# A streaming batch norm in which the third load no longer waits for the second

## Chip, cores, metric

The kernel runs on one core of a Trainium2 chip. The metric is device time in microseconds (us).

## The reference

```python
x: float32 [32, 256, 128, 128]; gamma, beta, running_mean, running_var: float32 [256]
return gamma * (x - mean) / np.sqrt(var + 1e-5) + beta     # one scale and one shift a channel
```

The data are 64 tiles of 128 partitions by 16384 float32, 8.39 MB each. Every tile is read once and written once.

## The kernel before

Three buffers hold three tiles. The sync queue issues the loads, the scalar queue the stores; VectorE computes each tile in place with one instruction. The first tile is loaded in two pieces, so that the parameters can pass between them. This is the part that matters, with cuts marked:

```python
nc.sync.dma_start(out=bufs[0][:, left], in_=xr[0][:, left]).then_inc(early, 16)
# ... four small loads of the parameters ...
nc.sync.dma_start(out=bufs[0][:, right], in_=xr[0][:, right]).then_inc(loaded[0], 16)
for i in range(1, NT):
    s, turn = i % NBUF, i // NBUF                       # NBUF = 3, NT = 64
    if turn:
        nc.sync.wait_ge(stored[s], 16 * turn)           # the buffer must have been stored
    inst = nc.sync.dma_start(out=bufs[s][:], in_=xr[i]).then_inc(loaded[s], 16)
    if i >= 2:                                          # the gate: the load before has landed
        inst._wait_ge(loaded[(i - 1) % NBUF], 16 * ((i - 1) // NBUF + 1))
# ... scale and shift from the parameters ...
compute(0, left)._wait_ge(early, 16)
compute(0, right)._wait_ge(loaded[0], 16)
store(0, 2)
for i in range(1, last):
    compute(i)._wait_ge(loaded[i % NBUF], 16 * (i // NBUF + 1))
    turn_of_store(i)                                    # store i-1 has landed
    store(i, i + 2)
compute(last, slice(0, VCOLS))._wait_ge(loaded[last % NBUF], 16 * turns)
nc.scalar.activation(out=t[:, VCOLS:], in_=t[:, VCOLS:], ...)   # the rest of the last tile
store(last, last + 3)                                   # without turn_of_store
```

## Time and profile before

| | before |
|---|---|
| time, median of 3 runs | 2486.41 us (2485.8 to 2487.24) |
| span in the profile | 2484.7 us |
| bytes moved, mean rate | 1073.84 MB, 432 GB/s |
| load 1 lands, load 2 is issued | 52.85, 52.87 us |
| load 2 lands | 91.50 us |
| store 0 lands (store 1 is issued then) | 69.8 us |
| last load lands, before the end of the span | 30.3 us |

In the lines of the profile q1 is the ring of the loads, q10 that of the stores. A line of the waits gives the total in us, the number of waits and the longest. A line of the timeline gives start, duration, engine or queue, source line and operation. The prediction below shows the lines of before and reads them.

### The profile page before, as it was taken

What the parts mean: (1) busy time and instruction counts of PE and PEld (TensorE: products, weight loads), DVE (VectorE), ACT (ScalarE), POOL (GpSimd) and SP (SyncE); (2) the same over time, 40 slices, a digit from 0 to 9 for tenths busy, and PEclk for the clock granted to TensorE, in tenths of its full rate; (3) what the DMA queues carried; (4) which work ended last, traced back from release to release, by engine and by line L of the source; (5) the groups of instructions that cost most, each with busy time, mean ns of one, the idle gap of its engine ahead of it and who ended that gap; (6) DMA issues with size and microseconds to landing.
All of it is one profiled execution on the core that took longest, in us unless ns stands there. A gap on an engine that the chain in (4) does not pass through costs nothing.

```text
span 2484.7 us, 389 instructions
## 1 busy us (share of the span) xinstructions
DVE 564.0 (23%) x76; ACT 7.9 (0%) x3; POOL 0.2 (0%) x4
## 2 busy tenths in 40 slices
DVE  3121221212212222122221221212212122121221
ACT  0000000000000000000000000000000000000001
POOL 0000000000000000000000000000000000000000
DMA  9999999999999999999999999999999999999999
GB/s 422 423 439 434 430 436 435 437 428 437 435 436 432 433 438 429 436 434 431 434 427 437 437 426 439 436 432 430 436 438 430 433 427 438 430 430 437 436 426 406
DMA packets 18707, 1073.84 MB, mean 432 GB/s; under 512 B 2128, under 2 KB 2192, under 8 KB 2192
## 3 DMA queue, kind: packets, MB, share of 16 engines
q1 hardware_dynamic: 9488, 536.94, 50.1%
q10 hardware_dynamic: 9216, 536.88, 49.9%
q14 instruction: 3, 0.02, 0.0%
HBM read 536.94 MB, written 536.87 MB: 432 GB/s over the span
## 4 chain that ended last, share of the span: by engine, by line
DMA 99%; ACT 0%; SPq 0%; issue 0%; DVE 0%; DVEq 0%
DMA t<-in_x_dram 99%; ACT t L154 0%; SPq L87 0%; DVE rows L85 0%; SPq L91 0%; DVE eps_t L103 0%; DVEq L190 0%; SPq L66 0%
## 5 line engine op out<-in xcount | busy, mean ns | idle before, releaser
L126 DVE TENSOR_SCALAR t<-t,scale_t,shift_t 128x16384 f32<-128x16384 f32 (+2 forms) x65 | 560.5, 8624 | 1886.5 <-DMA t<-in_x_dram 1886.4
L154 ACT ACTIVATE t<-t,shift_t,scale_t 128x7168 f32<-128x7168 f32 x1 | 6.4, 6361 | 2442.7 <-DMA t<-in_x_dram 2442.7
L104 DVE STREAM_TRANSPOSE turned<-rows 32x1024 f32<-32x1024 f32 x1 | 1.2, 1233 | 7.1 <-DMA rows<-in_running_mean_dram 7.1
L111 ACT ACT_TABLE_LOAD x1 | 1.3, 1283 | 0.9 <-SPq L66 0.9
L85 DVE MEMSET rows<- 32x1024 f32 x1 | 0.9, 912 | 1.2 <-SPq L66 1.2
L109 DVE COPY par<-turned 32x8 f32<-32x8 f32 x4 | 0.6, 162 | 0.1
L111 ACT ACTIVATE std_t<-par,eps_t 128x2 f32<-128x2 f32 x1 | 0.3, 295 | 9.2 <-DVE par L109 9.2
L118 DVE RECIPROCAL rstd_t<-std_t 128x2 f32<-128x2 f32 x1 | 0.2, 166 | 0.4 <-ACT std_t L111 0.4
L121 DVE TENSOR_TENSOR shift_t<-par,ms_t 128x2 f32<-128x2 f32 x1 | 0.2, 163 | 0.0
L120 DVE TENSOR_TENSOR ms_t<-par,scale_t 128x2 f32<-128x2 f32 x1 | 0.2, 161 | 0.0
L119 DVE TENSOR_TENSOR scale_t<-par,rstd_t 128x2 f32<-128x2 f32 x1 | 0.2, 161 | 0.0
L179 POOL MEMSET const-bfloat16-1.0<- 128x1 bf16 x1 | 0.1, 102 | 0.0
L179 POOL MEMSET const-uint8-127<- 128x1 uint8 x1 | 0.1, 101 | 0.0
L179 POOL MEMSET const-float32-0.0<- 128x1 f32 x1 | 0.1, 99 | 0.2 <-issue 0.2
L179 POOL MEMSET const-float32-1.0<- 128x1 f32 x1 | 0.1, 98 | 0.0
L103 DVE MEMSET eps_t<- 128x1 f32 x1 | 0.1, 59 | 0.1
## 6 DMA issues: line engine op xcount, KB each, us to landing
t<-in_x_dram SPq DMA_DIRECT2D x1, 6144.0 KB, 19.4
t<-in_x_dram SPq DMA_DIRECT2D x1, 2048.0 KB, 7.6
out_dram<-t ACTq DMA_DIRECT2D x64, 38.6
t<-in_x_dram SPq DMA_DIRECT2D x63, 38.6
rows<-in_running_var_dram SPq DMA_DIRECT2D x1, 16.0 KB, 6.4
rows<-in_gamma_dram SPq DMA_DIRECT2D x1, 16.0 KB, 6.2
rows<-in_beta_dram SPq DMA_DIRECT2D x1, 16.0 KB, 5.9
rows<-in_running_mean_dram SPq DMA_DIRECT2D x1, 16.0 KB, 5.9
```

The lines of the kernel that those rows point to most:

```text
L85: zeroed = step(nc.vector.memset(rows[:], 0.0))
L103: step(nc.vector.memset(eps_t[:], eps))
L104: step(nc.vector.transpose(out=turned[:], in_=rows[:]), fetched, 16 * NPAR)
L109: placed = step(nc.vector.tensor_copy(out=flat[q * B : (q + 1) * B], in_=blocks[:, :, q, 0]))
L111: nc.scalar.activation(out=std_t[:], in_=var_t, func=mybir.ActivationFunctionType.Sqrt, bias=eps_t[:], scale=1.0,)._wait_ge(vec, placed).t ...
L118: step(nc.vector.reciprocal(out=rstd_t[:], in_=std_t[:]), act, 1)
L119: step(nc.vector.tensor_mul(out=scale_t[:], in0=gamma_t, in1=rstd_t[:]))
L120: step(nc.vector.tensor_mul(out=ms_t[:], in0=mean_t, in1=scale_t[:]))
L121: ready = step(nc.vector.tensor_sub(out=shift_t[:], in0=beta_t, in1=ms_t[:]))
L126: return nc.vector.tensor_scalar(out=t[:, cols], in0=t[:, cols], scalar1=scale_t[:, cb : cb + 1], scalar2=shift_t[:, cb : cb + 1], op0=myb ...
L154: nc.scalar.activation(out=t[:, VCOLS:], in_=t[:, VCOLS:], func=mybir.ActivationFunctionType.Identity, bias=shift_t[:, cb : cb + 1], scale ...
L179: nc = _bacc.Bacc("TRN2", target_bir_lowering=False, num_devices=1)
```

## The change

Only loads into a buffer used before keep the gate: from load 3 (the fourth tile) on a load waits for the one ahead of it, while load 2 is queued directly behind load 1. The intent is to take a gap out of the ramp without giving up one transfer a ring in the steady state.

```diff
             inst = nc.sync.dma_start(out=bufs[s][:], in_=xr[i]).then_inc(loaded[s], 16)
-            if i >= 2:
+            if turn:
                 inst._wait_ge(loaded[(i - 1) % NBUF], 16 * ((i - 1) // NBUF + 1))
```

## The prediction

> **What bounds the kernel now.** I read the page first, then the chain of waits, the sync queue's own waits, the timeline of the first 180 us, and last the transfer records cut into stretches of one microsecond around 50 us.
>
> From the page:
>
> ```profile
> span 2484.7 us, 389 instructions
> DVE 564.0 (23%) x76; ACT 7.9 (0%) x3; POOL 0.2 (0%) x4
> ...
> DMA  9999999999999999999999999999999999999999
> GB/s 422 423 439 434 430 436 435 437 428 437 435 436 432 433 438 429 436 434 431 434 427 437 437 426 439 436 432 430 436 438 430 433 427 438 430 430 437 436 426 406
> ...
> q1 hardware_dynamic: 9488, 536.94, 50.1%
> q10 hardware_dynamic: 9216, 536.88, 49.9%
> ...
> DMA t<-in_x_dram 99%; ACT t L154 0%; SPq L87 0%; DVE rows L85 0%; SPq L91 0%; DVE eps_t L103 0%; DVEq L190 0%; SPq L66 0%
> ```
>
> The reader should see three things. The 16 transfer engines are busy in every one of the forty slices, while VectorE works 23% of the span. The two rings, q1 with the loads (sync queue) and q10 with the stores (scalar queue), take half of the engines each. And the chain that ended last is the loads alone, one after another. So the kernel is a stream of 1073.84 MB, and the time is those bytes by the rate, plus what is at the two ends.
>
> The sum, to know how much could be won at all. In the chain of waits the landings of two loads are most often 38.63 us apart; in that time one 8.39 MB tile is loaded and one is stored, 16.78 MB / 38.63 us = 434 GB/s. 64 tiles by 38.63 us are 2472.3 us. Before the first bytes lie 2.0 us and after the last ones some 3 us (the last stretches with traffic end at about 2481.5 us). The loads from 91.50 to 2454.41 us took 61 periods in 2362.91 us, where 61 x 38.63 would be 2356.4: some dozen periods were 38.8 to 39.4 us long, 6.5 us in all. 2472.3 + 2.0 + 3 + 6.5 = 2483.8, against a span of 2484.7. About 1 us is left over: the engines have no hole anywhere in which a saving could lie, in the ramp either.
>
> **The wait that the change removes.** The sync queue's own waits in the first 60 us, then the same kind of view for the whole span, then lines of the timeline:
>
> ```profile
> SPq L98 <- DMA t<-in_x_dram: 48.0, 1, 48.0
> ```
>
> ```profile
> SPq L98 <- DMA t<-in_x_dram: 1378.8, 62, 48.0
> SPq L97 <- DMA out_dram<-t: 1009.0, 61, 16.8
> ```
>
> ```profile
> 52.87 0.33 SPq L98 DMA_DIRECT2D t<-in_x_dram  x1
> ...
> 69.77 0.34 ACTq L137 DMA_DIRECT2D out_dram<-t  x1
> ...
> 91.52 0.33 SPq L98 DMA_DIRECT2D t<-in_x_dram  x1
> ```
>
> Load 2 (the third tile) waits 48.0 us for load 1 to land, at 52.85 us, and is issued at 52.87. It is the only one of the 62 waits at L98 that the change removes; 48.0 us looks large, but the sync queue has nothing else to do in them, and the engines were at work. Store 0 is issued at 30.04 us, lands at 69.7, and store 1 follows at once.
>
> What the wait costs the load ring is seen only in the transfer records. These are 16 packets of the load ring from 47 to 48 us, 16 of the store ring from 54 to 55 us, and the traffic from 44 to 62 us in forty slices of 0.45 us:
>
> ```profile
> q1 hardware_dynamic: 16, 1.05, 241.8%
> ```
>
> ```profile
> q10 hardware_dynamic: 16, 1.05, 241.8%
> ```
>
> ```profile
> GB/s 0 728 1602 0 0 0 146 2039 146 0 0 0 1602 728 0 0 0 728 1602 0 0 0 146 2039 146 0 0 0 1456 874 0 0 0 437 1893 0 0 0 0 1893
> ```
>
> 16 packets that take 241.8% of 16 engines' microsecond are 2.418 us each, of 65,536 bytes (1.05 MB / 16). The bursts of the last line, 2.4 us apart, are packets being booked where they end, all 16 engines in step. So time here comes in slots of 2.42 us, one packet per engine; a tile is 8 slots, and 16 slots are 38.7 us, the period. Going through the one-microsecond stretches, the slots end: load data 47.5, store 49.9, store 52.4 (with 16 empty packets of q1 in 51 to 53 us: load 1's semaphore), store 54.7, load 57. After its last data packet the load ring thus sits out two slots more than in plain turns: one in which the semaphore packet takes its turn, and one because load 2 is not yet in the ring at 52.4 us. In both the store ring moves a full packet on every engine.
>
> **What the Trainium skill says.** "DMA: Bandwidth & Descriptors", section "Queues, rings and completion order": each engine goes round-robin between the rings that have work, a packet at a time. This trace agrees, with alternating slots of 2.42 us where both have work, and one ring's packets alone where not. The same page, "Issuing engines are not separate DMA queues": transfers of the sync and scalar queues run on the same 16 engines and interleave; q1 at 50.1% and q10 at 49.9% say so too. Its section "Where 436 GB/s comes from" gives a ceiling of 435.2 GB/s; the 434 GB/s measured here lie 0.3% below. Its "Anatomy of one DMA" puts about 2 us of fixed cost on a transfer, mostly completion; that fits a semaphore that arrives a slot after the data, and it is a cost of the ring, not of the engines, as long as the other ring has packets.
>
> **The change, part by part.** It removes one wait, in one instruction; the instruction streams of all engines have the same rows in the same order in both kernels. The wait of load 2 alone goes; loads 3 to 63 keep both waits.
> 1. Load 2 is issued about 0.4 us after load 1, at some 4.8 us, rather than 52.87. Until load 1's data are done nothing changes: the load ring serves load 1 first.
> 2. At 52.4 us the load ring has a packet ready and takes the slot that store 0 has now. Gain for the load ring: 1 slot, 2.4 us. Loss for store 0: 1 slot, 2.4 us. Sum over the engines: 0.
> 3. Load 2 lands at 91.50 - 2.4 = 89.1 us, and store 0 at 69.7 + 2.4 = 72.1. Each ring starts its next transfer when its last has landed, so the shift stays: every later load lands 2.4 us earlier and every later store 2.4 us later than before.
> 4. Does this open a hole? Load 3 needs store 0 (72.1) and load 2 (89.1): the load still comes last. In the steady state the slack of the store wait was 21.8 us (the load landed that long after it); it becomes 21.8 - 4.8 = 17.0. Store 2 needs tile 2 computed (89.1 + 8.8 = 97.9) and store 1 landed (108.5 + 2.4 = 110.9): still no wait for VectorE. No hole.
> 5. The end: the last load lands at 2452.0 instead of 2454.4, the ScalarE and VectorE halves are done 6.4 us later, at 2458.4, and the last store enters the ring while store 62 still moves (it landed at 2464.1 before, and would at about 2466.5). Store 62 and 63 have then one slot more to move alone after the loads end. The 2.4 us won on the loads are handed back here, in full. Change of the end: 0.
>
> The sum is 0 us; I take off 0.1 us for one handover less, an allowance and no measurement, and predict 2486.3 us.
>
> **The rivals.** First: the slot is really saved, because the engines idle somewhere while the load ring is empty. It would make the time 2484.0 us. For it: the share of the engines swings from 0.15 to 1.5 in stretches of 2 us; but that is packets being booked in bursts, and from 52.85 to 91.50 us, which holds both gaps, 16.78 MB moved at 434 GB/s, as later. Against it too: after 2464 us the store ring alone moves a tile in 19.3 us, 434 GB/s, so one ring fills the engines. Second: the shift is harmful. If loads that ran ahead met a buffer not yet stored, each period would get longer; there are 17 us of slack by step 4, so nothing should come of it. Two loads queued in one ring could also spread the 16 engines apart, so that a transfer ends with its slowest engine and each handover costs more: half a slot in each of 61 periods would be 74 us, 3%. But load 1 was already queued directly behind the rest of tile 0, and the engines are in step within 1 us around 50 us. Third: the dozen long periods depend on how the two rings stand to each other; with none of them the time is 6.5 us less, with twice as many 6.5 us more. Nothing ties them to the phase, and I give it little weight.
>
> **Range and chances.** The three runs of before lie within 1.4 us; the first rival takes 2.4 us off; another sample of long periods may move 1 or 2 us. So 2484.0 to 2489.0 us. 2% are 50 us; nothing that the change touches is that large for the faster side, as only 12 us of the span are not packets at full rate. The slower side keeps a little for engines out of step.
>
> **What would show it.** In the changed kernel: the wait of 48.0 us at L98 gone and that line's waits 61; load 2 landing 2 to 3 us earlier and store 0 that much later; the wait for the store longer by about 5 us at each tile and for the load shorter by as much; the last load 2.4 us earlier and the span within 1.5 us. The prediction is wrong if the span falls by 2.4 us with the last load (then a slot was idle), if the periods differ from 38.6 us, or if the store ring does not lose the slot.

## The result, and the profile after

The changed kernel took 2485.47 us (median of 6 runs, 2483.91 to 2487.61) against 2486.11 us for before (6 runs, 2483.59 to 2487.33). The ratio is 0.9999, with a 95% interval of 0.9986 to 1.0012: the same. The interval is some 3 us wide to either side, so the times alone would not show a slot of 2.4 us, won or lost; that is left to the traces. Here and below a ratio is the mean time of one kernel's runs over that of the other's of the same rounds, so not quite the ratio of the medians quoted. Executions over 1.5% slower than the fastest of the same kernel are left out of the means.

From the page of the changed kernel:

```profile
span 2485.8 us, 389 instructions
...
DMA t<-in_x_dram 96%; DMA out_dram<-t 2%; DVE t L126 0%; ACT t L154 0%; SPq L87 0%; DVE rows L85 0%; DVE eps_t L103 0%; DVEq L190 0%; SPq L97 0%; SPq L66 0%
```

The bound is unchanged: the chain is still transfers end to end. It now passes through store 0 at its start, because load 3 waits for that store's landing before it waits for load 2. The profiled run of this kernel happened to be its slowest of six, so the 1.1 us between the two spans are not an effect.

**The ramp.** Timeline of the changed kernel, and then the two lines of before that the prediction does not show:

```profile
72.45 0.34 ACTq L137 DMA_DIRECT2D out_dram<-t  x1
...
89.36 0.33 SPq L98 DMA_DIRECT2D t<-in_x_dram  x1
...
111.16 0.34 ACTq L137 DMA_DIRECT2D out_dram<-t  x1
...
130.31 0.33 SPq L98 DMA_DIRECT2D t<-in_x_dram  x1
```

```profile
108.46 0.34 ACTq L137 DMA_DIRECT2D out_dram<-t  x1
...
130.20 0.33 SPq L98 DMA_DIRECT2D t<-in_x_dram  x1
```

Each issue follows the landing that it waits for by 0.02 to 0.1 us. Store 0 lands 2.7 us later than before (72.4 against 69.8) and load 2 lands 2.2 us earlier (89.34 against 91.50): one slot of 2.42 us has gone from one ring to the other. But load 3 lands at 130.29 us, 0.1 us later than before. In this pair of traces the lead in absolute time was gone after one tile (the second pair, below, differs).

Where it went is seen in the transfers. First the changed kernel from 54 to 55 us, where before 16 store packets stood; then the changed kernel from 93 to 94.2 us, and the kernel before from 92.9 to 94 us:

```profile
q1 hardware_dynamic: 14, 0.92, 211.6%
```

```profile
q1 hardware_dynamic: 13, 0.85, 164.0%
q10 hardware_dynamic: 3, 0.20, 48.0%
```

```profile
q10 hardware_dynamic: 16, 1.05, 219.8%
```

At 54 us the load ring takes the slot that store 0 had (the other two of its 16 packets start just after 55). At 93 us, the handover from load 2 to load 3, 13 engines already have a load packet and 3 do not: these take one more store packet. The engines have fallen into two groups. Load 3 has landed only when the slower group is done, so it lands nearly a slot late, and store 2 likewise (issued and landed 40.9 us apart instead of 38.7). The missed turn alone does not explain the delay. If each packet's end is joined to the start that follows it within 5 ns, the records can be followed engine by engine: the three engines make up the turn, with as many slots for load 3 as most of the others, but some of their packets take longer (on one of them 3.42, 2.76 and 3.12 us instead of 2.42; on another a store packet of 4.23). Why they do stays open.

**The steady state and the end.** The sync queue's waits over the whole span, after and then the two last of before:

```profile
SPq L97 <- DMA out_dram<-t: 1350.8, 61, 67.0
SPq L98 <- DMA t<-in_x_dram: 1035.6, 61, 19.2
SPq L164 <- DMA out_dram<-t: 50.4, 1, 50.4
SPq L66 <- DMA out_dram<-t: 19.3, 1, 19.3
```

```profile
SPq L164 <- DMA out_dram<-t: 48.0, 1, 48.0
SPq L66 <- DMA out_dram<-t: 19.3, 1, 19.3
```

The wait for the load is now 1035.6 / 61 = 17.0 us a tile; before it was (1378.8 - 48.0) / 61 = 21.8. The wait for the store grew from 1009.0 / 61 = 16.5 to (1350.8 - 67.0) / 60 = 21.4. So the two rings stand two slots otherwise to each other, through the whole run. At the end ScalarE starts on the last tile when its load has landed; before, then after:

```profile
2454.43 6.36 ACT t L154
```

```profile
2453.21 6.36 ACT t L154
```

From there to the end of the span are 2484.7 - 2454.4 = 30.3 us before and 2485.8 - 2453.2 = 32.6 us after. The store ring has one slot more to do alone. The slot that the load ring won is paid back at the end.

### The profile page after: what moved, and what is told of

It is laid out like the page before. It is cut to its first block, busy times and chain, and to the rows that moved or that the text cites. A ratio compares the mean times of both kernels' runs of the same rounds, so it can differ in the third digit from the quotient of the medians.

```text
span 2485.8 us, 389 instructions
## 1 busy us (share of the span) xinstructions
DVE 564.1 (23%) x76; ACT 7.9 (0%) x3; POOL 0.2 (0%) x4
## 4 chain that ended last, share of the span: by engine, by line
DMA 98%; another core or an unknown queue 1%; DVE 0%; ACT 0%; issue 0%; SPq 0%; DVEq 0%
DMA t<-in_x_dram 96%; DMA out_dram<-t 2%; DVE t L126 0%; ACT t L154 0%; SPq L87 0%; DVE rows L85 0%; DVE eps_t L103 0%; DVEq L190 0%; SPq L97 0%; SPq L66 0%
## 6 DMA issues: line engine op xcount, KB each, us to landing
out_dram<-t ACTq DMA_DIRECT2D x64, 38.6
t<-in_x_dram SPq DMA_DIRECT2D x63, 38.6
```

## Experiments

Twelve kernels ran; each was correct. Each group shared its runs of the kernel before. Edits are shown against the kernel before, with cuts marked.

### Controls: both kernels once more

Edit: none.

> The kernel before, unchanged, as a control. All theories: ratio 1.000, and single runs within 2483.5 to 2488. It tells how large a difference has to be before a time can show it, and whether the store lands 17 us after the load in a second trace too.

> The changed kernel, unchanged, for a second trace. Theory (the slot of 2.42 us passes from the store ring to the load ring and is handed back at the end): within 1.5 us of before; load 2 lands at 89 to 90 us, store 0 at 72 to 73, and the last load lands about 31 us before the end of the span instead of 30.3 less a slot. Rival (a slot is saved for good, and the first trace hid it by chance): 2.4 us faster. If the 3 engines that missed their turn at load 3 in the first trace are chance, load 3 lands at 127.8 us here; if they are the rule, at about 130.3 again.

| | median us | runs | ratio, 95% interval |
|---|---|---|---|
| kernel before, shared | 2484.04 | 9 | |
| before_again | 2484.28 | 5 | 0.9998 (0.9984 to 1.0011) |
| after_again | 2484.67 | 5 | 0.9999 (0.9987 to 1.0012) |

The handover from load 2 to load 3 in the second trace of the changed kernel:

```profile
89.22 0.33 SPq L98 DMA_DIRECT2D t<-in_x_dram  x1
...
128.54 0.33 SPq L98 DMA_DIRECT2D t<-in_x_dram  x1
```

And the landing of load 3 in the second trace of the kernel before:

```profile
131.43 0.33 SPq L98 DMA_DIRECT2D t<-in_x_dram  x1
```

Load 2 and store 0 (72.3 us) do the same as in the first trace. Load 3 lands at 128.5 us, between the two values expected: from 93 to 94.2 us, 10 engines took a load packet and 6 a store packet. In a third trace with the same ramp (slow_tail_after below) it was 13 and 3 again. So the split at load 3 is in all three traces of this ramp, and its size varies. The kernel before is not free of it: in its first trace 14 load and 2 store packets start from 56 to 58 us, where load 2 begins, and had caught up when load 2 landed; in its second trace two engines lag at load 3, which lands at 131.4 us, 1.2 us later than in the first. Pair by pair, load 3 of the changed kernel is then 0.1 us late, 2.9 us early here, and 1.0 us early in the slow tails (129.2 against 130.1). What does not vary is the relation of the rings: from the last load's landing to the end of the span, 2484.1 - 2453.8 = 30.3 us in before_again and 2482.8 - 2450.1 = 32.7 us here. The rival of a slot saved for good is out.

### slow_tail_before, slow_tail_after: let the end hang on the last load

ScalarE alone computes the last tile, so that the last store comes after the store ring has run empty. The same edit on both kernels:

```diff
-        compute(last, slice(0, VCOLS))._wait_ge(loaded[last % NBUF], 16 * turns)
         nc.scalar.activation(
-            out=t[:, VCOLS:],
-            in_=t[:, VCOLS:],
+            out=t[:],
+            in_=t[:],
...
-        store(last, last + 3)
+        store(last, last + 2)
```

> The kernel before, with ScalarE alone computing the last tile, about 14.5 us instead of 6.4: the last store is issued some 4 us after the store ring has run empty. Theory: the end now hangs on the last load's landing; about 7 us longer than before, 2491 to 2495.

> The same with the changed kernel. Theory: the load ring's one slot of lead, handed back at the end otherwise, is now seen: 2.4 us (1 to 4) less than the same tail on the kernel before, about 2489 to 2492. Rival (the lead of 2.4 us does not live to the end): the same time as with the tail on the kernel before.

With this tail the kernel before took 2489.55 us (5 runs, 2488.23 to 2490.42; ratio 1.0021, 1.0007 to 1.0034) and the changed kernel 2487.30 us (5 runs, 2486.74 to 2489.48; ratio 1.0014, 1.0000 to 1.0029). The wait between the landings of the last two stores, which was 19.3 us in both, first with the kernel before and then with the changed one:

```profile
SPq L66 <- DMA out_dram<-t: 25.1, 1, 25.1
```

```profile
SPq L66 <- DMA out_dram<-t: 22.7, 1, 22.7
```

The hole at the end is 25.1 - 19.3 = 5.8 us in one and 22.7 - 19.3 = 3.4 us in the other: a difference of one slot, 2.4 us. The medians differ by 2.25 us, the means by 1.7; the traces are the firmer of the two. The total for the kernel before was lower than the 2491 us expected at least, as ScalarE took 14.04 us and the hole was 5.8 us, not 7. The lead does live to the end, and is worth 2.4 us in a kernel whose end hangs on its last load. In the real kernel the end hangs on bytes.

### gate_first: put a wait where nothing else can fill it

```diff
-            if i >= 2:
+            if i >= 1:
```

> Load 1 too waits for the load before it, at 23.3 us, when no store is in the store ring yet (store 0 is issued at 30 us). Theory (a wait costs what the engines stand idle): a hole from the last packet of tile 0 to the first of load 1, about 1.5 to 3.5 us, and the whole run that much longer: 2487.5 to 2490. Rival (a wait between two loads costs nothing, or one slot, wherever it is): 0, or 2.4 us, and no stretch without traffic at 23 to 26 us in the trace.

It took 2488.83 us (5 runs, 2487.49 to 2491.0; ratio 1.0019, 1.0007 to 1.0032). The traffic from 20 to 30 us in slices of 0.25 us, of the kernel before and then of this one:

```profile
GB/s 0 0 1180 1769 197 0 0 0 0 1049 2359 786 0 0 0 0 0 0 0 1573 2621 0 0 0 0 0 0 0 524 1835 1835 0 0 0 0 0 0 0 1049 2359
```

```profile
GB/s 0 0 1573 1573 0 0 0 0 0 0 0 0 0 0 0 0 2097 1573 262 0 262 0 0 0 0 0 0 0 262 2884 1049 0 0 0 0 0 0 0 1311 2359
```

The packets are booked where they start. The last packet of tile 0 starts at 20.5 to 21 us in both. By the records the first of load 1 follows at 22.36 us before and only at 24.15 us here: a hole of about 1.8 us. It is the same kind of wait as the one that the change removed, ahead of the neighbouring load, and it costs time because the store ring is empty until 30 us. The time rose by 4.8 us between the medians, more than the hole. Another 0.6 us are at the end, where the last store waited 19.9 us instead of 19.3, and in the records the first packets of load 1 take 3.14 us on average instead of 2.42, which is 0.7 us more. These 3.1 us are about what the span of this trace, 2487.1 us, lies above the two traces of before (2484.7 and 2484.1); the rest of the 4.8 us is not accounted for (see the next run).

### hold_part: hold load 2 back further, beside a busy store ring

```diff
-            if i >= 2:
+            if i == 2:
+                inst._wait_ge(done, 3)
+            elif i > 2:
                 inst._wait_ge(loaded[(i - 1) % NBUF], 16 * ((i - 1) // NBUF + 1))
...
+            if i == 1:
+                compute(1, slice(0, 6144))._wait_ge(loaded[1], 16)
+                compute(1, slice(6144, HW))
+            else:
+                compute(i)._wait_ge(loaded[i % NBUF], 16 * (i // NBUF + 1))
```

(The counts of `done` that later stores wait for go up by one.)

> Load 2 is held back further: it waits until a first part of tile 1 has been computed, 3.3 us after load 1 has landed. Theory: the store ring fills the slots (store 0 lands one or two slots earlier, load 2 one or two later, at 93 to 97 us), no hole, the time within 1.5 us of before. Rival (the wait of load 2 lies on the path to the end): 3.3 us or one to two slots, 2.4 to 4.8 us, longer.

It took 2487.74 us (6 runs, 2484.73 to 2499.62) against 2484.30 us; ratio 1.0022, 1.0003 to 1.0042. Timeline, and the last wait:

```profile
64.94 0.34 ACTq L139 DMA_DIRECT2D out_dram<-t  x1
...
96.51 0.33 SPq L98 DMA_DIRECT2D t<-in_x_dram  x1
```

```profile
SPq L66 <- DMA out_dram<-t: 19.9, 1, 19.9
```

Store 0 lands 4.8 us earlier than in before (two slots) and load 2 lands 5.0 us later, as the theory has it. The time missed what it expected: the medians differ by 3.4 us, which by size would fit the rival. The trace does not show where 3.4 us would lie. Its span is 2484.9 us, against 2484.7 and 2484.1 in the two traces of before, with traffic in every slice and 0.6 us at the end. It does not rule a loss out either: the runs of before in the same rounds had spans of 2481.2 to 2484.4 us. The slowest runs, one of them at 2499.62 us, were not profiled. In this kernel and in gate_first the stores land about 12 us after the loads (706.8 / 61 and 714.1 / 61 us of wait for the store), not 17 or 22. The next runs show that this distance can matter; that it costs 2 to 3 us here is not shown and stays open.

### no_gate: take the gate away altogether

```diff
-            if i >= 2:
-                inst._wait_ge(loaded[(i - 1) % NBUF], 16 * ((i - 1) // NBUF + 1))
```

> No load waits for the load before it; loads 3 to 63 wait for their buffer's store alone. Theory (engines always have a packet, so who waits in a ring does not matter): loads run ahead by one slot a tile until the store of the buffer holds them, and the time stays within 3 us of before. Rival one (each gap in the load ring costs a slot of the span): 61 gaps less, up to 61 x 2.42 = 148 us faster, 6%. Rival two (when the store's landing starts both the next load and the next store, both rings are empty at once): a hole of about 2 us a tile, some 50 x 2 = 100 us slower, 4%.

It took 3225.88 us (5 runs, 3216.49 to 3232.75): ratio 1.2983 (1.2960 to 1.3006), 30% slower. No theory had this size. From its page, and then its transfers from 60 to 150 us alone:

```profile
GB/s 418 432 361 315 337 322 319 348 317 336 315 339 323 316 337 314 341 317 357 322 319 338 314 345 319 334 316 315 336 315 350 314 335 317 326 336 315 340 317 360
...
q1 hardware_dynamic: 9488, 536.94, 47.8%
q10 hardware_dynamic: 9216, 536.88, 40.9%
```

```profile
DMA packets 656, 38.80 MB, mean 431 GB/s; under 512 B 64, under 2 KB 64, under 8 KB 64
```

The rate is full for the first two slices and then falls to some 330 GB/s for good. In the full-rate part a second load is queued behind the first about half of the time (from 5 to 53, 72 to 89, 113 to 126 and 155 to 162 us). From 72 us on each landing of a store releases the next load and the next store together. At first an earlier load is then still in the ring; the rate falls from 204 us on, when the loads have run so far ahead that this ring too is empty at that moment (the load landed at 203.85 us, the store at 204.0). Two things are added up in the 740 us. The engines stand without work for 100 - 47.8 - 40.9 = 11% of the span, some 360 us, about half. And the single packets take longer: in the trace's records from 204 us on, load packets average about 3.06 us and store packets 2.58 us where they were 2.42 us.

### store_two_back: release a load and a store together another way

```diff
             if turn:
-                nc.sync.wait_ge(stored[s], 16 * turn)
+                nc.sync.wait_ge(stored[(i - 2) % NBUF], 16 * ((i - 2) // NBUF + 1))
```

> Each load from the fourth on waits for the store two tiles back, not three, as if there were two buffers. The load and the next store are then released by the same landing, when both rings have run empty. Theory (a wait costs only when both rings are empty): a hole of 1.5 to 3 us at each of some 61 tiles, 2580 to 2670 us, 4 to 7% slower. Rival (the engines' work is what counts and waits do not matter): within 2%.

It took 3000.51 us (median of 4; 2876.7, 3002.09, 3005.1 and 2998.92), beyond the 7% expected. Only the first of these counts as fast, so no ratio was formed; at a clock of 1.0 in all four, the two patterns of the rings (below) may be the reason for the spread, which the one trace can't show. The first stretch below is from 300 to 1700 us, the second from 1800 to 2800 us of the profiled run, which was the one of 2876.7 us:

```profile
DMA packets 8579, 499.15 MB, mean 357 GB/s; under 512 B 960, under 2 KB 960, under 8 KB 960
```

```profile
DMA packets 6768, 394.27 MB, mean 394 GB/s; under 512 B 752, under 2 KB 752, under 8 KB 752
```

It found two patterns and changed from one to the other near 1700 us. In the first every other pair of load and store starts together (packets of some 3.0 us for the load), and in the pairs between them the store starts 8.6 us after the load (2.7 us). In the second the store starts 1.6 and 6.4 us after the load in turn (2.63 us for the load, 2.42 for the store). The holes that I expected are there, but the stretched packets came on top. That the rate changes with how load and store stand to each other in time is thus seen within one run.

### in_phase: a common start, with one transfer a ring

The kernel before with its gate, and one more wait ahead of stores 1 to 62:

```diff
             turn_of_store(i)
+            nc.scalar.wait_ge(loaded[(i + 1) % NBUF], 16 * ((i + 1) // NBUF + 1))
             store(i, i + 2)
```

> The kernel before, with its gate on the loads, and each store but the first and last waiting for the next tile's load to land, so that a load and a store start together in their rings, one transfer in each. Theory (starting together, in phase, is what stretches the packets to some 3.06 and 2.58 us, not the depth of the queue): some 50 us a tile, 3050 to 3350 us. Rival (two loads queued in one ring are the cause): packets of 2.42 us and a hole of about 2 us a tile, 2550 to 2650 us.

It took 3242.50 us (4 runs, 3239.28 to 3245.06): ratio 1.3049 (1.3027 to 1.3071). Rings, from its page:

```profile
q1 hardware_dynamic: 9488, 536.94, 48.0%
q10 hardware_dynamic: 9216, 536.88, 40.7%
```

These are no_gate's figures to 0.2 points, and load packets again take about 3.06 us and store packets 2.58. Past the start there is never a second load in the ring here. So a deep queue is not needed for the slow state; a load and a store that are released together into empty rings, and run in phase, are enough. By what means they stretch the packets is not shown.

### Three runs on the rows: inconclusive

The last three asked whether load and store going over the same rows of their tiles at the same time is what stretches the packets. Each store is cut into four of 32 rows:

```diff
-            inst = nc.scalar.dma_start(out=outr[i], in_=bufs[s][:]).then_inc(stored[s], 16)
-            inst._wait_ge(done, after)
+            nc.scalar.wait_ge(done, after)
+            for r0 in (0, 64, 32, 96):          # in_phase_rows_same; (32, 96, 0, 64) in the other two
+                nc.scalar.dma_start(out=outr[i][r0 : r0 + 32], in_=bufs[s][r0 : r0 + 32]).then_inc(stored[s], 16)
```

(The counts of `stored` are 64 a tile instead of 16. apart_rows_other is the kernel before with this edit alone; the other two have in_phase's wait too.)

> As in_phase, with each store cut into four of 32 rows, in the order 0, 64, 32, 96, meant to be the order in which a whole load goes over the rows. A control for the next run. All theories: about as in_phase; the cut itself costs up to three turns of a ring a tile and no engine time, so within 5% of in_phase.

> As the control, with the four parts of each store in the order 32, 96, 0, 64: load and store start together and go over different rows of their tiles. If the stretch comes of load and store going over the same rows at the same time: packets of some 2.42 us, 2500 to 2700 us. If it comes of the common start itself, or anything that does not know rows: as the control, within 5%.

> The kernel before, gate and all, without the common start, with each store cut into four in the order 32, 96, 0, 64. Stores run about half a tile behind loads, so this order brings load and store to the same rows at the same time. If same rows at the same time are the cause: packets stretched to 2.6 to 3.1 us, 2750 to 3300 us. If the common start is: within 1% of before.

They took 3457.87, 3233.38 and 3236.53 us (2 runs each), 1.39, 1.30 and 1.30 of before. The control missed its 5% (6.6% over in_phase), and the last wait of in_phase_rows_same shows why none of the three can decide:

```profile
SPq L66 <- DMA out_dram<-t: 33.4, 1, 33.4
```

The last store, with nothing beside it, now takes 33.4 us where a whole one takes 19.3. Stores of 32 rows are slow by themselves (33.4 and 33.6 us in the other two runs), so the runs measure the cut. There is a second fault: with the slower stores, apart_rows_other did not stay apart. From 252 us on its load and store start together, as these lines of its timeline show, so that it tests the common start once more:

```profile
1049.14 2.20 ACTq L139 DMA_DIRECT2D out_dram<-t  x4
1049.18 0.33 SPq L98 DMA_DIRECT2D t<-in_x_dram  x1
```

What stretches packets in phase stays open.

No run beat both kernels. The spread of the controls, 0.14%, is larger than anything that the ramp has to give.

## Why the prediction was right, point by point

- **The bound and the empty budget**: held. The time is bytes by rate, and the engines of the changed kernel have work in every slice.
- **Step 1 and 2, one slot from store 0 to load 2**: held. Load 2 landed at 89.34 us (89.1 forecast) and store 0 at 72.4 (72.1).
- **Step 3, every later load 2.4 us earlier and every later store 2.4 us later**: the relation held, the absolute times did not. Load 3 was at +0.1 us in the first trace instead of -2.4, as 3 of 16 engines missed their turn and then had longer packets. In the other two pairs of traces it was 2.9 and 1.0 us ahead; the kernel before itself had it at 130.2 and 131.4 us in two traces. The prediction had taken the engines for one body in step; a landing is that of the slowest group. What it forecast for the waits, 17.0 us for the load and some 5 us more for the store, came out as 17.0 and 4.9.
- **Step 4, no hole**: held, but the reason given was incomplete. It looked only at slack.
- **Step 5, the slot handed back at the end**: held, at 30.3 against 32.6 us from the last load to the end, and shown by the slow tails, where the 2.4 us reappear.
- **First rival, the slot really saved**: out, by the longer end in both traces and by the slow tails. The two ratios of 0.9999 agree, but their intervals would not exclude 2.4 us.
- **Second rival, engines out of step**: it does happen, in the kernel before too: at 57 us, where the prediction reads a slot of load data with all engines in step, 2 of 16 still start a store packet. The missed turn costs no work, since the engine takes a store packet instead; longer packets on such engines cost nearly a slot of landing time in the first trace.
- **Third rival, the rate depends on how the rings stand to each other**: put aside too lightly. "Nothing ties them to the phase" is wrong in general: with a common start the kernel is 30% slower. The runs show the full rate with the stores 12 us (gate_first, hold_part), 17 and 22 us behind the loads in a period of 38.6 us, and a lower one with 0 us, and with 0 and 8.6 or 1.6 and 6.4 us in turn. The change moved them from 17 to 22, within the good range; that this, and not the slack of 17 us, made it safe is argued from these figures and not tested.
- **A reading that failed**: the prediction took packets to be booked where they end. The records in the trace have a start and a duration, and the views count by start. The order of the slots, on which the working rests, is the same either way, but each of its slot times is a start, 2.42 us before the end. So the turn that load 2 missed came at 54.3 us, after its issue at 52.87 and not before it; and the last packet ends at 2483.0 us, 1.6 us before the end of the span and not 3, which leaves 2.3 us instead of 1 in the prediction's sum. That the engines had no hole rests on the transfer records, not on this remainder.

## What to carry to other kernels

A wait of 48 us in a queue is worth what the engines behind it stand idle, and here they never did: the other ring took each slot. Before valuing a removed wait, follow the slot it frees to the end of the kernel and see who gives it back. And do not take a gate between large transfers away for good because lifting it once was harmless: here it also kept loads and stores from being released together into empty rings, and taking it away altogether cost 30%.

## What the Trainium skill lacked or had wrong

- "DMA: Bandwidth & Descriptors", section "Issuing engines are not separate DMA queues", says that transfers of several queues interleave, and not that their relation in time changes the rate. Here one load and one store of 8.39 MB move at 434 GB/s together when 17 us apart, and at some 330 GB/s when they start together (packets of 3.06 and 2.58 us for 2.42).
- The same page's "Queues, rings and completion order" gives turns of a packet. Its order agrees; here a turn was 65,536 bytes and 2.42 us, so a ring that comes late loses that much, and engines can miss it singly (3, 6 and 3 of 16 in three traces). No page has the splitting of engines into groups.
- The same page's "Latency and other measured facts" has a first byte after some 600 ns. With empty rings that fits: load 1 of gate_first, issued from 23.18 to 23.53 us, had its first packet at 24.15. Beside a busy store ring, load 2 of the kernel before, issued at 52.87 us, did not get the turn at 54.3 to 54.9 us, 1.4 us later at least.
